# GpSimd's tensor work moved to VectorE and ScalarE, and the mixer's weights split by DMA, in a hybrid encoder layer

## The chip, the cores and the metric

The kernel runs on one core of a Trainium2 chip. The metric is the device time in microseconds, the median of three runs. The profile is one execution, taken by the hardware profiler; its times count from the first instruction.

## The reference

One layer over 512 tokens of width 1024, in float32: an input projection whose columns feed latent attention (four heads) and a gated linear recurrence in both directions (four heads, HGRN2), an output projection, a gated feed-forward of width 2816, and a gate with per-layer embeddings.

```python
h = rms_norm(x, g_mix[l]); z = h @ w_in[l]
c_q, c_kv, k_r, hq, hf_f, hf_b, hi, hg = jnp.split(z, IN_SPLITS, axis=-1)   # 256, 256, 64, then five of 512
a = mla(c_q, c_kv, k_r, cos, sin, ...)      # norms, w_qb, w_kvb, rotary parts, dense softmax
r = hgrn2(hq, hf_f, hf_b, hi, hg, ...)      # chunkwise scan per direction, chunks of 64, summed, normed, gated
x = x + jnp.concatenate([a, r], axis=-1) @ w_o[l]
h = rms_norm(x, g_ffn[l])
x = x + (silu(h @ w_gate[l]) * (h @ w_up[l])) @ w_down[l]
x = x + sigmoid(rms_norm(x, g_ple[l]) @ w_ple_gate[l]) * (p[l] @ w_ple_proj[l])
```

## The kernel before

Every large product runs as three float32r matmuls on TensorE: operands are split into a high and a low part, and `mm3` (L136 to L139) adds high x high, low x high and high x low into one PSUM bank. A chunk of weights, 128 rows by up to 1024 columns (512 KB), goes through `weights` (L143):

```python
sp.dma_start(raw[:, :cols], src)                                              # L149
split(hi[:, :cols], lo[:, :cols], raw[:, :cols], eng=lo_eng or dve)           # L150
# split without a scale:
act.activation(hi, src, AF.Copy)                                              # L130
eng.tensor_tensor(lo, src, hi, ALU.subtract)                                  # L131
```

Buffers: four raw (`RAWB`), three high and three low (`WB`). `split` with a scale (L133, L134) does the same for x and other activations on ScalarE and VectorE.

The work goes in this order.

1. *Latents of the query* (`cq`, L223): blocks of 128 features of x, eight of them, arrive one after the other with the columns of `w_q`; per block six matmuls of 512 columns. Seven warm-up matmul calls stand ahead. GpSimd sums the squares of x (L244, L246).
2. *Latents of key and value* (`ckv`, L251): a second pass over the eight blocks with `w_kv`, twelve matmuls of 320 columns per block. Then `token_rstd` makes 1/rms by token (its power runs on GpSimd, L164).
3. *Rotary tables* (L275 to L299) on GpSimd, the sines on ScalarE.
4. *Two streams side by side* (`merge`): each is a generator that yields TensorE's time piece by piece, and the one that is behind its share emits next. The latency stream has `attention()` (L329) and then the steps in the written order `LSTEPS`: per head `prepare`, `scores`, `values` of the attention, and `decays`, `within`, `carried`, `outputs`, `finish` of the recurrence. The dense stream (L868) has the input projection's other columns: `gates` for heads 0 and 1, then 2 and 3 (L598), the values (`w_in_tokens`, evacuated in L665), the embeddings, `output_gates` (L650), then half of the output projection and the embeddings' product. Its weights come through `wnext` (L560), 30 chunks in all, with one chunk ahead of use; of the first 14 every second one makes its low part on GpSimd. PSUM has eight banks, five for the latency stream and three for the dense one.
5. *The second half of the output projection, feed-forward, embeddings gate* (from L936): `weights` straight, from about 300 us to the end.

`gates(heads)` ends in a burst: sigmoids on ScalarE of six tiles of 128x512, then on VectorE f = lower + (1 - lower) sigmoid (L616), k = 1 - f (L618), two clamped copies (L627, L628), logarithms on ScalarE (L631), their sum on GpSimd (L634) and a scan on VectorE (L636, L638). `decays` has on GpSimd the distance to a chunk's middle (L681) and two products of half a tile (L698, L699). `within(h)` makes the products inside chunks, `pd` (L729), in pairs for a tile's two chunks, and per direction the one from a tile's earlier chunk to its later one, `px` (L731):

```python
for d in range(2):
    for j in range(NT):
        for c in range(2):
            pe.matmul(pd4[c * 64 : c * 64 + 64, d, j, :], ...)                # L729
        pe.matmul(px3[E * 64 : E * 64 + 64, j, :], lhsT=kx[:, j, :], ...)     # L731, E = d
```

The order of instructions on an engine is set by a planner at build time from the program's order and a simulated timeline; every engine works its list in order.

Of the kernel before, what the change touches and what calls it, by code (L numbers as in the profile page):

```python
# [8 lines left out]
F32 = mybir.dt.float32  # L9
# [6 lines left out]
P = 128  # L16
# [38 lines left out]
class Slots:  # L55
    """Tiles of one size, handed out by hand: the one that has been free longest comes next."""
# [57 lines left out]
def layer_kernel(ctx: ExitStack, tc: tile.TileContext, io, out):  # L114
# [44 lines left out]
    def rsqrt_mean(o, ss, n):  # L159
        """o = (ss / n + eps) ** -0.5, for a few columns."""  # L160
# [14 lines left out]
        # the diagonal matrices of 1 / rms, summed over the partitions  # L175
# [13 lines left out]
    def squares(acc, src, first):  # L189
        """acc += src ** 2"""  # L190
# [8 lines left out]
    # ---------------------------------------------------------------- inputs  # L199
# [3 lines left out]
    sp.dma_start(vec, io["vec"])  # L203
# [7 lines left out]
    # loads the activation engine's table while the first inputs are under way  # L211
    act.activation(small.tile([P, 1], F32, tag="first", name="first"), mhalf[:, :1], AF.Exp)
# [10 lines left out]
    for ks in ((0,), (1,), (2, 3), (4, 5), (6, 7)):  # L223
        w = weights(io["w_q"][:, ks[0] * 256 : (ks[-1] + 1) * 256], len(ks) * 256)
        for k in ks:
            if k:
                sp.dma_start(xT[k], io["xT"][k])
            split(hT[k][0], hT[k][1], xT[k], vec[:, V_MIX + k : V_MIX + k + 1])
            for m in range(2):
                o = (k - ks[0]) * 256 + m * P  # L230
                mm3(cq[m], cut(w, o, o + P), hT[k], k == 0, k == KT - 1)

    cst = cpool.tile([P, NC_], F32, name="cst")
    sp.dma_start(cst, io["cst"])
    row = cpool.tile([P, NR], F32, name="row")
    sp.dma_start(row, io["row"].partition_broadcast(P))
# [842 lines left out]
```

## Time and profile before

| | us |
|---|---|
| median of three runs (723.8 to 726.64) | 723.89 |
| profiled execution, span | 721.8 |
| TensorE busy | 703.6 (97%) |
| VectorE busy | 439.3 (61%) |
| ScalarE busy | 309.2 (43%) |
| GpSimd busy | 135.8 (19%) |

The page gives no other time of the profiled execution than its span. Matmuls are pipelined, so busy TensorE is not TensorE at its peak; the granted clock is near 1.0 in nearly all slices. PE is TensorE, PEld its weight loads, DVE VectorE, ACT ScalarE, POOL GpSimd, SP the engine that issues the transfers.

### The profile page before, as it was taken

How to read it: one execution, taken by the hardware profiler on the slowest of the kernel's cores; microseconds unless marked ns; L12 is line 12 of the kernel's file. 1: busy time of each engine (PE TensorE's matmuls, PEld its weight loads, DVE VectorE, ACT ScalarE, POOL GpSimd, SP SyncE). 2: the span in 40 equal slices, each digit the busy share in tenths (PEclk: the TensorE clock that was granted, in tenths of full speed). 3: DMA queues.
4: the chain of work that ended last, by engine and by line, in shares of the span. 5: the costliest groups of instructions: out<-in, count | busy, mean ns of one | idle time of the engine just before them, and what ended most of it. 6: DMA issues, size and time to landing. Idle time of an engine off the chain costs nothing.

```text
span 721.8 us, 9167 instructions
## 1 busy us (share of the span) xinstructions
PE 703.6 (97%) x3516; PEld 588.5 (82%) x3516; DVE 439.3 (61%) x733; ACT 309.2 (43%) x573; POOL 135.8 (19%) x126
## 2 busy tenths in 40 slices
PE   8999997998999999999999999999999999999997
PEld 6888885897878888788888888888888888888886
DVE  8954469988999984386545334435433444456573
ACT  5566785576554635355233222223222223244341
POOL 7983577010543511001000000000000000000000
PEclk9999999999999999999999999999999999999999
DMA  8432112111034221033232322232233232233211
GB/s 282 167 114 93 59 36 81 59 30 60 15 103 156 60 78 59 30 118 116 96 109 87 104 101 87 91 114 77 79 108 117 90 108 87 78 105 116 89 59 58
DMA packets 22075, 66.36 MB, mean 92 GB/s; under 512 B 2704, under 2 KB 3984, under 8 KB 22032
## 3 DMA queue, kind: packets, MB, share of 16 engines
q1 hardware_dynamic: 22032, 65.79, 28.0%
q8 instruction: 27, 0.44, 0.2%
q14 instruction: 16, 0.13, 0.1%
HBM read 63.68 MB, written 2.10 MB: 91 GB/s over the span
## 4 chain that ended last, share of the span: by engine, by line
PE 85%; DVE 8%; ACT 3%; DMA 2%; issue 1%; SPq 1%; POOL 0%; ACTq 0%; POOLq 0%
PE ff L137 11%; PE ff L138 11%; PE ff L139 11%; PE dn L138 6%; PE dn L137 6%; PE dn L139 6%; PE wi L139 3%; PE wi L137 3%; PE wi L138 3%; PE pg L139 2%; PE pg L138 2%; PE pg L137 2%; PE wo L137 2%; PE wo L139 2%; PE wo L138 2%; PE po L787 1%
## 5 line engine op out<-in xcount | busy, mean ns | idle before, releaser
L130 ACT ACTIVATE whi<-raw 128x1024 fp32r<-128x1024 f32 (+4 forms) x114 | 116.2, 1019 | 286.6 <-issue 103.1
L131 DVE TENSOR_TENSOR wlo<-raw,whi 128x1024 fp32r<-128x1024 f32 (+4 forms) x108 | 133.7, 1240 | 26.1 <-ACT whi L130 24.8
L137 PE MATMUL ff<-hh,whi 128*128 128x512 f32 x352 | 137.0, 390 | 0.1
L138 PE MATMUL ff<-hl,whi 128*128 128x512 f32 x352 | 136.8, 389 | 0.0
L139 PE MATMUL ff<-hh,wlo 128*128 128x512 f32 x352 | 136.8, 389 | 0.0
L957 DVE TENSOR_TENSOR z<-ff,rsbc 128x512 f32<-128x512 f32 x44 | 30.1, 691 | 109.8 <-PE ff L139 109.2
L164 POOL TENSOR_TENSOR rs_tok<-rs_v,mhalf 128x4 f32<-128x4 f32 x3 | 4.7, 1568 | 391.7 <-DVE rs_v L163 391.7
L137 PEld LDWEIGHTS ff<-hh,whi 128*128 128x128 f32 x352 | 66.1, 188 | 14.3 <-ACT whi L130 0.5
L138 PEld LDWEIGHTS ff<-hl,whi 128*128 128x128 f32 x352 | 66.1, 188 | 13.7
L139 PEld LDWEIGHTS ff<-hh,wlo 128*128 128x128 f32 x352 | 66.1, 188 | 13.6
L137 PE MATMUL dn<-ah,whi 128*128 128x512 f32 x176 | 68.5, 389 | 0.0
L138 PE MATMUL dn<-al,whi 128*128 128x512 f32 x176 | 68.5, 389 | 0.0
L139 PE MATMUL dn<-ah,wlo 128*128 128x512 f32 x176 | 68.5, 389 | 0.0
L139 PE MATMUL wi<-hh,wlo 128*128 128x512 f32 x128 | 51.7, 404 | 3.6 <-DVE wlo L131 3.6
L926 DVE TENSOR_TENSOR x<-x,dn 128x512 f32<-128x512 f32 x24 | 16.5, 687 | 60.5 <-PE dn L139 60.5
L138 PE MATMUL wi<-hl,whi 128*128 128x512 f32 x128 | 51.4, 401 | 0.0
L137 PE MATMUL wi<-hh,whi 128*128 128x512 f32 x128 | 51.0, 400 | 0.0
L137 PEld LDWEIGHTS dn<-ah,whi 128*128 128x128 f32 x176 | 33.0, 188 | 6.9
L139 PEld LDWEIGHTS dn<-ah,wlo 128*128 128x128 f32 x176 | 33.0, 188 | 6.8
L138 PEld LDWEIGHTS dn<-al,whi 128*128 128x128 f32 x176 | 33.0, 188 | 6.8
L139 PEld LDWEIGHTS wi<-hh,wlo 128*128 128x128 f32 x128 | 24.5, 191 | 8.9 <-DVE wlo L131 4.0
L138 PEld LDWEIGHTS wi<-hl,whi 128*128 128x128 f32 x128 | 24.4, 191 | 4.9
(287 smaller groups left out, 1361.9 us busy)
## 6 DMA issues: line engine op xcount, KB each, us to landing
raw<-in_w_gate SPq DMA_DIRECT2D x22, 512.0 KB, 3.3
raw<-in_w_up SPq DMA_DIRECT2D x22, 512.0 KB, 3.2
raw<-in_w_hf SPq DMA_DIRECT2D x16, 512.0 KB, 3.7
raw<-in_w_d SPq DMA_DIRECT2D x16, 448.0 KB, 3.2
x<-in_xT SPq DMA_DIRECT2D x16, 256.0 KB, 5.2
raw<-in_w_d SPq DMA_DIRECT2D x8, 512.0 KB, 3.3
raw<-in_w_pg SPq DMA_DIRECT2D x8, 512.0 KB, 3.2
raw<-in_w_i SPq DMA_DIRECT2D x4, 512.0 KB, 3.4
```

The lines of the kernel that those rows point to most:

```text
L130: act.activation(hi, src, AF.Copy)
L131: eng.tensor_tensor(lo, src, hi, ALU.subtract)
L137: pe.matmul(o, lhsT=l[0], rhs=r[0], start=start, stop=False)
L138: pe.matmul(o, lhsT=l[0], rhs=r[1], start=False, stop=False)
L139: pe.matmul(o, lhsT=l[1], rhs=r[0], start=False, stop=stop)
L164: pool.tensor_tensor(o, v[:, :w], mhalf[:, :w], ALU.pow)
L787: pe.matmul(po[:, ts(j)], lhsT=l, rhs=r, start=n == 0, stop=n == len(terms) - 1)
L926: dve.tensor_tensor(xT[m], xT[m], o, ALU.add)
L957: dve.tensor_tensor(z, o, bc2, ALU.mult)
```

## The change

- *GpSimd's tensor operations* go to VectorE: the rotary products of key and query, `q` times its sigmoid, the sum of logarithms, the distance to the chunk's middle, qx and kx. The squares of x are ScalarE's, their sum VectorE's. The rotary tables and the norms' powers stay on GpSimd.
- *From VectorE to ScalarE*: the evacuation of the values and the first copy of each carried state. The scale of the scores is multiplied into the query's norm, the maximum comes out negated, and the query's gains are multiplied into rotary tables of its own (`ccq`, `snq`): one operation less each time.
- *Weights of the mixer*: from the third of the 30 chunks on, GpSimd's queue issues a transfer with a cast into the high part, ScalarE writes minus the high part into the low one, and a second transfer adds the source onto it. Three chunks are asked for ahead instead of two; four high and low buffers, three raw ones. Feed-forward keeps the old way.
- *Latents together*: per block of x the weights of query and key-value come into one buffer, and the key-value matmuls of the block follow the query's; those of the last two blocks stand behind `token_rstd`. The constants are loaded in parts at other places, the rotary tables are made after the second block, ten warm-up calls instead of seven.
- *Tables*: the activation table sets are loaded by name: trigonometry first, then one set with exp and ln behind the sines and behind each group of sigmoids.
- *px in pairs*: the two directions' px of a tile are issued one behind the other.
- The dense stream emits its first four pieces ahead of the latents' evacuation.

```diff
-AHEAD = 2
-WB = 3
-RAWB = 4
+AHEAD = 3
+WB = 4
+RAWB = 3
-WARM = 7
+WARM = 10
-LO_POOL = 14
+LO_DVE = 2
+FIRST = 4
...
+        if by_dma:
+            pool.dma_start(hi[:, :cols], src)
+            act.activation(lo[:, :cols], hi[:, :cols].bitcast(F32), AF.Copy, scale=-1.0)
+            pool.dma_start(lo[:, :cols], src, accum_op=ALU.add)
+        else:
+            raw = wpool.tile([P, 1024], F32, tag="raw", bufs=RAWB, name=f"raw{nw[0]}")
+            sp.dma_start(raw[:, :cols], src)
+            split(hi[:, :cols], lo[:, :cols], raw[:, :cols])
...
+    act.preload_act_table_set("trig_and_small")
+    def exp_ln():
+        return act.preload_act_table_set("natural_log_exp_and_others")
...
+    def load_k(k):
+        if k:
+            sp.dma_start(xT[k], io["xT"][k])
...
+        sp.dma_start(raw[:, :256], io["w_q"][:, k * 256 : k * 256 + 256])
...
+        sp.dma_start(raw[:, 256:576], io["w_kv"][:, k * 320 : k * 320 + 320])
+        for c in (slice(0, 256), slice(256, 576)) if k == 0 else (slice(0, 576),):
+            split(hi[:, c], lo[:, c], raw[:, c])
+            if c.start == 0:
+                split(hT[k][0], hT[k][1], xT[k], vec[:, V_MIX + k : V_MIX + k + 1])
+        ws.append((hi, lo))
...
     for k in range(KT):
-        t = A.get("sq") if k else sq
-        pool.tensor_tensor(t, xT[k], xT[k], ALU.mult)
-        if k:
-            pool.tensor_tensor(sq, sq, t, ALU.add)
-            A.put(t)
...
+        load_k(k)
+        query_k(k)
+        if k == 1:
+            rotary_tables()
+        squares(sq, xT[k], k == 0)
+        if k < KT - 2:
+            key_k(k)
...
     rs1, bc1 = token_rstd(sq, cpool)
     A.put(sq)
+    for k in range(KT - 2, KT):
+        key_k(k)
+    BD = B.part("D", 2)
...
-            dve.tensor_scalar(rq, rq, sq_, None, ALU.mult)
+            dve.tensor_scalar(rq, rq, sq_, QK_SCALE, ALU.mult, ALU.mult)
...
-            pool.tensor_tensor(x, x, row[:, R_QN : R_QN + 64].unsqueeze(1).broadcast_to([P, H, 64]), ALU.mult)
-            rope(pool, x, x, cc[:, j : j + 1].broadcast_to([P, H, 64]),
-                 sn[:, j : j + 1].broadcast_to([P, H, 64]), t4, t8)
+            rope(dve, x, x, ccq[:, j : j + 1].broadcast_to([P, H, 64]),
+                 snq[:, j : j + 1].broadcast_to([P, H, 64]), t4, t8)
...
-            on_pool = nd[0] % 2 == 0 and nd[0] < LO_POOL
-            ahead.append(weights(*wlist.popleft(), pool if on_pool else dve))
+            ahead.append(weights(*wlist.popleft(), by_dma=nd[0] > LO_DVE))
...
-        together([lambda o=o, z=z: act.activation(o, z, AF.Sigmoid) for o, z in reversed(fs)])
+        together([lambda o=o, z=z: act.activation(o, z, AF.Sigmoid) for o, z in reversed(fs)], exp_ln)
...
-            pool.tensor_tensor(q[h], q[h], sg[h], ALU.mult)
+            dve.tensor_tensor(q[h], q[h], sg[h], ALU.mult)
...
-            pool.tensor_tensor(f, f, t, ALU.add)
+            dve.tensor_tensor(f, f, t, ALU.add)
...
-        dve.tensor_scalar(vv[j][:, cols], o, rs1[:, j : j + 1], None, ALU.mult)
+        act.activation(vv[j][:, cols], o, AF.Copy, scale=rs1[:, j : j + 1])
...
-            pool.tensor_tensor(v3(t1, 8), b3, bc8(b3[:, :, mid : mid + 1]), ALU.subtract)
+            dve.tensor_tensor(v3(t1, 8), b3, bc8(b3[:, :, mid : mid + 1]), ALU.subtract)
...
-            pool.tensor_tensor(qx, c4(e1)[:, :, L], bc4(dc[:, 0, :, L]), ALU.mult)
-            pool.tensor_tensor(kx, c4(e2)[:, :, E], bc4(dc[:, 1, :, E]), ALU.mult)
+            dve.tensor_tensor(qx, c4(e1)[:, :, L], bc4(dc[:, 0, :, L]), ALU.mult)
+            dve.tensor_tensor(kx, c4(e2)[:, :, E], bc4(dc[:, 1, :, E]), ALU.mult)
...
+            for d in range(2):
+                qx, kx = decayed[h, d][5:7]
+                pe.matmul(px3[d * 64 : d * 64 + 64, j, :], lhsT=kx[:, j, :], rhs=qx[:, j, :], start=True, stop=True)
...
+    dense = dense_stream()
+    for _ in range(FIRST):
+        next(dense)
...
+    BL = B.part("L", NBL)
+    BD.join(B)
```

## Rows read from the trace of the kernel before

**Rows 1.** Windows: stretch, its us, busy us and (count) by engine, clock, DMA, GB/s.

```profile
5.30:36.70 31.40, 28.56 (x147) 24.61 (x147) 29.91 (x29) 17.95 (x29) 30.20 (x25) 1.00 0.70 236
...
100.00:126.00 26.00, 21.41 (x91) 16.75 (x90) 24.95 (x32) 17.95 (x30) 20.37 (x14) 0.93 0.18 58
154.00:180.00 26.00, 23.22 (x147) 20.59 (x146) 21.86 (x48) 19.04 (x33) 3.81 (x3) 0.93 0.13 42
180.00:216.00 36.00, 34.59 (x234) 28.80 (x233) 33.70 (x68) 20.23 (x39) 17.91 (x13) 1.00 0.19 59
100.00:260.00 160.00, 151.18 (x932) 126.83 (x931) 149.59 (x313) 97.39 (x189) 60.91 (x46) 0.98 0.21 67
36.70:306.60 269.90, 261.04 (x1517) 219.84 (x1517) 202.17 (x432) 159.41 (x380) 100.75 (x92) 0.99 0.22 69
306.60:680.00 373.40, 373.37 (x1653) 309.36 (x1653) 181.03 (x227) 117.51 (x147) 1.93 (x1) 1.00 0.31 99
```

**Rows 2.** Timeline of 0 to 25 us: start, us, engine, line, operation, [idle before <- releaser].

```profile
1.04 3.35 PE L221 MATMUL warm<-ones 128*128 128x128 f32 x14 [1.04 <-DVE ones L206]
...
4.68 0.74 DVE L134 SCALAR_TENSOR_TENSOR hl<-x,vec,hh 128x512 fp32r<-128x512 f32 x1
...
8.90 0.63 PE L138 MATMUL cq<-hl,whi 128*128 128x512 f32 x1
...
9.33 0.63 PE L139 MATMUL cq<-hh,wlo 128*128 128x512 f32 x1
...
13.88 3.20 DVE L134 SCALAR_TENSOR_TENSOR hl<-x,vec,hh 128x512 fp32r<-128x512 f32 x2
...
15.69 0.50 PE L138 MATMUL cq<-hl,whi 128*128 128x512 f32 x1 [1.49 <-DVE hl L134]
...
24.05 0.31 PE L139 MATMUL ckv<-whi,hl 128*128 128x320 f32 x1
...
24.49 0.31 PE L139 MATMUL ckv<-whi,hl 128*128 128x320 f32 x1
```

**Rows 3.** The chain of waits, 96 to 126 and 154 to 216 us: start, us, what.

```profile
102.70 3.99 DVE z L616 x2
...
113.78 2.22 DVE wlo L131
...
176.41 1.28 ACT L631
```

**Rows 4.** Timeline of 102 to 108 us, GpSimd.

```profile
103.89 2.52 POOL L131 TENSOR_TENSOR wlo<-raw,whi 128x1024 fp32r<-128x1024 f32 x1
```

**Rows 5.** Groups by line, VectorE, 100 to 260 us: xcount | busy us, mean ns | idle before.

```profile
L131 DVE TENSOR_TENSOR wlo<-raw,whi 128x1024 fp32r<-128x1024 f32 x14 | 19.8, 1417 | 0.3 <-ACT whi L130 0.2
...
L616 DVE TENSOR_SCALAR z<-z,lower,lower 128x512 f32<-128x512 f32 x8 | 8.2, 1062 | 2.6 <-ACT z L613 2.6
...
L576 DVE TENSOR_TENSOR z<-wi,rsbc 128x512 f32<-128x512 f32 x10 | 6.7, 681 | 0.3 <-PE pT L529 0.2
...
L665 DVE TENSOR_SCALAR v<-wt,rs_tok 128x256 f32<-128x256 f32 x8 | 3.8, 475 | 2.0 <-PE av L138 1.9
...
L627 DVE TENSOR_SCALAR t<-z 128x512 f32<-128x512 f32 x8 | 3.2, 417 | 0.0
```

**Rows 6.** Groups by line, ScalarE, 36.7 to 306.6 us.

```profile
L130 ACT ACTIVATE whi<-raw 128x1024 fp32r<-128x1024 f32 x29 | 30.7, 1058 | 27.7 <-PE wo L138 10.1 <-PE wi L138 8.2 <-issue 5.8
```

**Rows 7.** Timeline of 256.2 to 257.5 us, TensorE.

```profile
256.94 0.28 PE L731 MATMUL px<-xx 128*64 128x64 f32 x2
257.06 0.28 PE L729 MATMUL pd<-e,e 128*64 128x64 f32 x2
```

**Rows 8.** DMA issues: xcount, KB each, median us to landing.

```profile
raw<-in_w_hf SPq DMA_DIRECT2D x16, 512.0 KB, 3.7
```

**Rows 9.** Groups by line, GpSimd, whole span.

```profile
L634 POOL TENSOR_TENSOR z<-z,t 128x512 f32<-128x512 f32 x8 | 13.5, 1702 | 21.9 <-ACT t L631 21.9
...
L244 POOL TENSOR_TENSOR sqacc<-x 128x512 f32<-128x512 f32 x1 | 1.0, 1038 | 2.0 <-DMA x<-in_xT 2.0
```

More of the change, by code (lines that the diff above doesn't have):

```diff
@@ L235, in layer_kernel, with together @@
     row = cpool.tile([P, NR], F32, name="row")
-    sp.dma_start(row, io["row"].partition_broadcast(P))
     pos = cpool.tile([P, NT], I32, name="pos")
-    sp.dma_start(pos, io["pos"])
     ident = cst[:, C_ID : C_ID + P]
+    ckv = [B.get(f"ckv{j}") for j in range(NT)]
+    ws = []
+    cc = cpool.tile([P, NT, 64], F32, name="cc")
+    sn = cpool.tile([P, NT, 64], F32, name="sn")
+    def together(emit, last=None):
+        es = [emit[0]()]
+        with tc.issue_after(es[0].ins):
+            for e in emit[1:]:
+                es.append(e())
+        if last:
+            with ExitStack() as behind:
+                for e in es:
+                    behind.enter_context(tc.issue_after(e.ins))
+                last()
@@ new lines, in rotary_tables @@
+    def rotary_tables():
+        posf = small.tile([P, NT], F32, tag="posf", name="posf")
+        pool.tensor_copy(posf, pos)
+        ang, rnd, tmp = (A.get(n) for n in ("ang", "rnd", "tmp"))
+        freq = cst[:, C_FREQ : C_FREQ + 32]
+        a3, n3, t3 = (t[:, : NT * 32] for t in (ang, rnd, tmp))
+        for j in range(NT):
+            pool.tensor_scalar(a3[:, j * 32 : j * 32 + 32], freq, posf[:, j : j + 1], None, ALU.mult)
+        pool.tensor_scalar(n3, a3, 1.0 / TWO_PI, None, ALU.mult)
+        pool.tensor_scalar(n3, n3, MAGIC, None, ALU.add)
+        pool.tensor_scalar(n3, n3, MAGIC, None, ALU.subtract)
+        for c in (CW1, CW2, CW3):
+            pool.tensor_scalar(t3, n3, c, None, ALU.mult)
+            pool.tensor_tensor(a3, a3, t3, ALU.subtract)
+        pool.tensor_scalar(a3, a3, 3.1415925, -3.1415925, ALU.min, ALU.max)
+        ang3 = a3.rearrange("p (a b) -> p a b", a=NT)
+        act.activation(t3, a3, AF.Abs)
+        pool.tensor_scalar(t3, t3, -1.0, TWO_PI / 4, ALU.mult, ALU.add)
+        tmp3 = t3.rearrange("p (a b) -> p a b", a=NT)
+        together([lambda: act.activation(cc[:, :, :32], tmp3, AF.Sin),
+                  lambda: act.activation(sn[:, :, 32:], ang3, AF.Sin),
+                  lambda: act.activation(sn[:, :, :32], ang3, AF.Sin, scale=-1.0)], exp_ln)
+        pool.tensor_copy(cc[:, :, 32:], cc[:, :, :32])
+        A.put(ang, rnd, tmp)
@@ L258, in layer_kernel @@
+        squares(sq, xT[k], k == 0)
+        if k < KT - 2:
+            key_k(k)
+    sp.dma_start(cst[:, :C_FREQ], io["cst"][:, :C_FREQ])
+    sp.dma_start(row, io["row"].partition_broadcast(P))
+    vlb = cpool.tile([P, 16], F32, name="vlb")
+    sp.dma_start(vlb, io["vec"][:, V_LB : V_LB + 16])
+    A.put(*xT)
     rs1, bc1 = token_rstd(sq, cpool)
     A.put(sq)
-    cT = [None] * 4
-    sqc = A.get("sqc")
-    for m in range(2):
-        cT[m] = (A.get("cTh", F32R), A.get("cTl", F32R))
-        split(cT[m][0], cT[m][1], cq[m], vec[:, V_QA + m : V_QA + m + 1])
-        squares(sqc, cq[m], m == 0)
@@ L267, in layer_kernel @@
-    B.put(*cq)
-    ctok = [A.get(f"c{j}") for j in range(NT)]
-    for j in range(NT):
-        act.copy(ctok[j][:, :320], ckv[j][:, :320])
-    B.put(*ckv)
-    BL, BD = B.part("L", NBL), B.part("D", 8 - NBL)
-    posf = small.tile([P, NT], F32, tag="posf", name="posf")
-    pool.tensor_copy(posf, pos)
-    ang, rnd, tmp = (A.get(n) for n in ("ang", "rnd", "tmp"))
-    freq = cst[:, C_FREQ : C_FREQ + 32]
-    a3, n3, t3 = (t[:, : NT * 32] for t in (ang, rnd, tmp))
-    for j in range(NT):
-        pool.tensor_scalar(a3[:, j * 32 : j * 32 + 32], freq, posf[:, j : j + 1], None, ALU.mult)
@@ L641, in gates @@
             done.add(("gates", h))
-    def together(emit):
-        first = emit[0]()
-        with tc.issue_after(first.ins):
-            for e in emit[1:]:
-                e()
     def output_gates():
@@ L655, in output_gates @@
         t = [A.get("sg") for h in range(H)]
-        together([lambda h=h: act.activation(t[h], zs[h], AF.Sigmoid) for h in reversed(range(H))])
+        together([lambda h=h: act.activation(t[h], zs[h], AF.Sigmoid) for h in reversed(range(H))], exp_ln)
         for h in range(H):
@@ L919, in layer_kernel @@
     wlist.extend((io["w_or"][c], 1024) for c in range(4))
-    merge([(latency_stream(), L_TOTAL), (dense_stream(), D_TOTAL)])
+    dense = dense_stream()
+    for _ in range(FIRST):
+        next(dense)
+    cT = [None] * 4
+    sqc = A.get("sqc")
+    for m in range(2):
+        cT[m] = (A.get("cTh", F32R), A.get("cTl", F32R))
+        split(cT[m][0], cT[m][1], cq[m], vec[:, V_QA + m : V_QA + m + 1])
+        squares(sqc, cq[m], m == 0)
+    B.put(*cq)
+    ctok = [A.get(f"c{j}") for j in range(NT)]
+    for j in range(NT):
+        act.copy(ctok[j][:, :320], ckv[j][:, :320])
+    B.put(*ckv)
+    BL = B.part("L", NBL)
+    BD.join(B)
+    merge([(latency_stream(), L_TOTAL), (dense, D_TOTAL - 1.3 * FIRST)])
     A.put(mF, *ats, *vv)
```

93 lines of the change are left out of this document (36 added, 57 removed).

## The prediction

> **What bounds the kernel now.** I read the windows by stage first, then the chain of waits inside the stages with losses, then the groups by line of the engine that the chain names, then the timeline where two engines collide. From 306.6 us on TensorE is busy without a gap: 1653 matmuls in 373.4 us, 0.226 us each, nearly all 512 columns wide [rows 1]. That stage is feed-forward, its instructions are not changed, and it returns nothing. What the change can touch lies in the first 306.6 us, and the reader is to see there how little of it is loss.
>
> The front, 5.3 to 36.7 us, holds 48 query-latent matmuls of 512 columns and 96 key-value ones of 320. At 0.226 us and 0.147 us (the latter from three starts, 24.05 to 24.49 us [rows 2]) that is 10.8 + 14.1 = 24.9 us of work in 31.4 us; 6.5 us are lost. Two causes stand in [rows 2]: at 9 us consecutive 512-column matmuls still start 0.43 us apart, which is the clock at 1.2 GHz, after a first stretch of warm-up calls with gaps behind them, and later TensorE waits 1.49 us for the low part of x that VectorE makes.
>
> The second loss is 100 to 216 us. Idle TensorE time is 26.00 - 21.41 = 4.6, 26.00 - 23.22 = 2.8 and 36.00 - 34.59 = 1.4 us, 8.8 together; and in the first two of these stages the granted clock averages 0.93, which takes 7% of 26 us, 1.8 us, from each [rows 1]: the clock fell to 1.2 GHz for a while after TensorE had waited. Sum 12.4 us. The chain of waits there runs over VectorE: two gate operations that hold it 3.99 us, a low part of weights that holds it 2.22 us [rows 3]. The timeline beside it says why they are long: GpSimd's own low part of weights runs from 103.89 for 2.52 us, to 106.41, and VectorE's two gate operations get done at 106.69, right behind it [rows 3, 4]. The same kind of gate arithmetic takes 0.42 us in another line [rows 5]. So VectorE, 149.6 of 160 us busy from 100 to 260 us [rows 1], is the engine that ends last there, and part of its busy time is waiting for GpSimd.
>
> **The change, part by part.** *Front.* Weights for query and key-value come per block of x, so that one block feeds 6 x 0.226 + 12 x 0.147 = 3.1 us of TensorE work at once instead of 1.4. VectorE then has per block a low part of 576 columns (0.77, from 0.68 at 512 wide [rows 5]), a low part of x (0.74 without contention: the smallest I see in the stretch; with it 1.60, half of the 3.20 us that two take [rows 2]) and the new square sum (0.68): 2.2 us, 3.1 with contention. ScalarE has three passes of 512 to 576 columns, of which the squares were GpSimd's before; one of 1024 columns takes 1.06 [rows 6], so I count 0.65 each, 2.0 us. TensorE stays the slowest of the three. Transfer: 256 + 288 KB per block at the 236 GB/s of this stretch [rows 1] is 2.4 us, also below 3.1. The rotary tables move forward on GpSimd, where squares no longer stand, and collide with VectorE during about four blocks; constants, row and positions are loaded a few issues later or earlier on SP, with 25 us of TensorE work as cover. The first block still pays its chain, and the three extra warm-up calls (six records of 0.24 us, 3.35 us for 14 [rows 2]) end about when the first weights arrive, so that start stays near 5.3 us. I take 2.5 us of the 6.5 as staying and 4.0 us as gain; bounds 1.5 (only the wait of 1.49 goes) and 6.0.
>
> *VectorE from 100 to 260 us.* Away go 14 low parts of weights (19.8), 8 value evacuations (3.8, now ScalarE's), the contention in the gate operations, 8 x (1.06 - 0.42) = 5.1 [rows 5], and small scalings that I don't count: 28.7 us. To it come GpSimd's 20 operations of 128x512 with two inputs at 0.68 = 13.6 and 16 of half that width at 0.45 = 7.2 (between a half and a whole one): 20.8 us. Net -8 us, 5% of 149.6, and no GpSimd tensor work beside it. The rotary products move to VectorE too, but before 100 us; outside 100 to 260 us it is busy 202.2 - 149.6 = 52.6 of 109.9 us of this part [rows 1], which hides them; without that cover each of the query's four tiles would add four operations, under 0.45 us each, 1.8 us. The loss of 100 to 126 us (4.6 + 1.8) is nearly all contention: 3.99 - 2 x 0.42 = 3.2 and 2.22 for the weight part that is no longer there, 5.4 us of chain. I give back 6.0 of 6.4. In 154 to 216 us, 6.0 us, GpSimd is little in the way (3.81 busy in 26 us [rows 1]) and the chain is VectorE's own; one of its pieces, a table load of 1.28 us for the logarithm, goes because exp and ln now share one set, loaded right behind the sigmoids [rows 3]. I give back half, 3.0. Together 9.0; bounds 3 (VectorE as full as before, only the two collisions of the first burst gone) and 12.4 (all).
>
> *px in pairs.* The px matmuls of one tile are now issued for both directions next to each other and write different halves of the partitions, as the pd pairs do already. A px call takes 0.12 us before the next pd starts [rows 7]; 32 calls, half saved: 1.9 us. Bounds 0 (hidden behind VectorE) and 1.9.
>
> *Weights by DMA.* 28 of the 30 chunks of the mixer now come by two transfers on GpSimd's queue with a ScalarE pass between: cast to the high part, minus the high part into the low one, then the source added onto it. ScalarE pays what it paid (1.06 for the high part before [rows 6]), VectorE nothing. The new waits: the adding transfer waits on GpSimd's queue for ScalarE's pass, and behind it there stand the next chunk's cast and the power operations of every norm (12 after 40 us), for which VectorE and then ScalarE's evacuations wait; the ScalarE pass waits for the cast's landing, and exponentials and PSUM evacuations stand behind it. No row shows a transfer from GpSimd's queue. Nearest is the same 512 KB by SP, 3.7 us to landing [rows 8]. Low end of one chunk's turn on the queue: 3.7 + 1.06 + two issues of 1.0 (as GpSimd's 128x512 operation alone, 1.04 [rows 9]) = 6.8 us. High end: each issue is held by VectorE as GpSimd's sums of logarithms are now (1.70 instead of 1.04 [rows 9]) or by a whole collision, seen from the other side (2.2 us of GpSimd's 2.52, taken as the other way round), and ScalarE is 1 us late: 12.2 us. Needed is a chunk every 269.9 / 28 = 9.6 us [rows 1], and 5.4 us (24 x 0.226) where TensorE has only dense work, before 57 us; there four buffers give three chunks, 16 us, of lead. I take 8 us: enough over the stretch, short by some 2.6 us for the first one or two chunks. Cost 2.0; bounds 0 and, if the turn is over 9.6 us, the rival below.
>
> A rule of the Trainium skill speaks against this part: its page "SBUF — State Buffer" (sections "SBUF: two separate sides" and "A bandwidth-pool intuition that's wrong") says that a transfer issued by GpSimd has its descriptors written by that engine, which is locked out of SBUF while VectorE runs an operation in a two-port mode, and gives about 0.6 us alone and 3.1 us beside one for such a transfer. No run here shows such a transfer yet; that the two engines hold each other up the trace agrees with (2.52 beside 3.99 us). By it, an estimate, each chunk's turn would be longer by 2 x 2.5 us, 11.8 instead of 6.8.
>
> **Sum.** 721.8 - 4.0 - 9.0 - 1.9 + 2.0 = 708.9 us for the profiled execution. The page shows no time of it but the span; the median of the runs, 723.9, is 2.1 above, which I add: **711 us**.
>
> **Rivals.** *VectorE stays the bound.* It takes on 20.8 us of GpSimd's work, and the bursts behind each sigmoid keep their length; the front gives 3.0, the middle 3.0, px 0 because it waits for VectorE, and 2.0 is paid: 717.8, 720 us with the 2.1. For it: 93% busy, and the chain of 154 to 216 us, where GpSimd is quiet; against it: the 8 us less and the two collisions that go. *GpSimd's queue becomes the bound.* Cast, wait, add, in order, longer than 9.6 us: at 10.6, 28 us over 28 chunks on top of 708.9, 739 us; it decides from about 10.1, where 0.5 x 28 = 14 us eat all gain. For it: the collisions in [rows 4], in the stretch where VectorE is fullest; against: the low end of 6.8, and that casts can be queued ahead of adds. The rule of the Trainium skill named above is this case. *TensorE alone bounds.* Every loss of the middle goes, front 6.0, px 1.9, no new wait: 721.8 - 12.4 - 6.0 - 1.9 + 2.1 = 704 us; for it, nothing but the full queues of TensorE elsewhere.
>
> **Chances.** Forecast (706 to 717) 0.58, VectorE stays 0.20, GpSimd's queue 0.13, TensorE alone 0.09. Half a per cent, 3.6 us, is about what a measurement of this kernel can tell from no change: 720.3 to 727.5. The second case straddles the lower edge, a half each side. Faster 0.58 + 0.09 + 0.10 = 0.77, same 0.10, slower 0.13. The range takes in the forecast and the two cases beside it, down to 702 (TensorE alone, with stalls shorter than a row shows) and up to 722 (VectorE stays, with 2 us more); outside is the third.
>
> **What would show it.** The profile after should have the first dense matmuls at about 33 us instead of 37; the gate operation at 0.4 to 0.6 us instead of 1.06; no TensorE stretch with granted clock below 1.0 around 116 us; VectorE below 140 us busy in the stretch that answers to 100 to 260; weight adds on GpSimd's queue less than 9.6 us apart. The forecast is wrong if TensorE waits for the low weights by name, if ScalarE idles for a landing with exponentials behind it, or if the middle's loss stays above 8 us.

## The result and the profile after

The changed kernel takes 717.29 us (median of four runs, 716.77 to 717.76), the kernel before 723.85 on the same chip: ratio 0.9897, 95% interval 0.9878 to 0.9917. It is faster by 1.0%, twice what a measurement can tell from no change. The forecast was 711 us: sign right, inside the range of 702 to 722, 0.3 us over the forecast's own band of 706 to 717, and of 12.8 us forecast 6.6 came. The profiled execution took 717.26 us with a span of 715.5.

The windows of the changed kernel, by stage (columns as in [rows 1]; the first row answers to the front, the second and third to the two bursts):

```profile
5.30:34.10 28.80, 26.93 (x155) 24.13 (x154) 24.24 (x43) 22.23 (x39) 9.91 (x18) 1.00 0.83 268
100.00:126.00 26.00, 26.00 (x123) 21.52 (x122) 25.12 (x74) 17.17 (x34) 6.77 (x9) 1.00 0.70 148
150.00:172.00 22.00, 18.16 (x88) 13.92 (x87) 20.50 (x42) 13.14 (x27) 0.00 (x0) 0.84 0.00 1
220.00:240.00 20.00, 19.38 (x100) 16.01 (x100) 15.32 (x31) 14.54 (x30) 5.19 (x7) 1.00 0.59 150
240.00:260.00 20.00, 17.53 (x167) 13.83 (x166) 14.28 (x30) 6.60 (x19) 4.11 (x6) 1.00 0.65 131
100.00:260.00 160.00, 153.07 (x987) 128.12 (x986) 127.77 (x305) 92.50 (x189) 26.28 (x35) 0.98 0.54 122
305.00:680.00 375.00, 375.00 (x1663) 310.83 (x1663) 180.02 (x230) 114.83 (x141) 3.01 (x2) 1.00 0.30 97
```

The reader is to see three things. The front is shorter and nearly full: the first dense matmul starts at 33.81 us, where it started at 37.50. From 100 to 126 us TensorE is busy without a gap at clock 1.00, where it was idle 4.6 us at 0.93 [rows 1]; VectorE is as busy there as before (25.12 of 26 us). From 150 to 172 us TensorE loses 3.8 us to idleness and runs at 0.84, and hardly a byte moves (1 GB/s); at 240 to 260 it loses 2.5 us more.

Idle time and clock can be put into one number: the time between the starts of consecutive matmuls, less the time which a matmul of that width takes in full stretches of the same trace (0.227 us for 512 columns, 0.174 for 384, 0.147 for 320, 0.118 for 256, 0.108 for 128, 0.05 for 64). Summed by stretch, in us, with e1 to e12 for the kernels of the next section (`whole` also has what lies behind 310 us, between -0.5 and 0.5):

```
stretch   before  changed   e1     e2     e4     e7     e8    e11    e12
0-50        9.1     5.8     3.9    5.3    3.6   12.7    5.5    3.2    4.8
50-100      0.4     0.4     0.4    0.3    0.4    0.4    0.4    0.4    0.4
100-150     7.5     0.4     1.4    1.5    1.0    0.4    7.9    0.4    0.7
150-180     5.3     9.1    12.5   12.2    7.9    8.8    8.4    7.2   10.1
180-220     3.6     1.3     1.2    0.9    1.3    0.1    2.7    1.6    1.6
220-310     2.5     4.4     5.5    4.2    4.3    1.2    4.2    2.2    4.0
whole      27.9    21.0    24.6   24.9    18.2   23.2   28.8   14.7   21.3
```

The changed kernel loses 6.9 us less and has six more warm-up records (0.65 us): 6.3, which is the difference of the spans, 721.8 - 715.5. By 150 us it has gained 10.4 us of lost time. Behind that it gives back 3.4.

**What the second burst looks like.** VectorE of the changed kernel, 146 to 170 us (start, us, engine, line, operation):

```profile
147.87 1.29 DVE L655 TENSOR_TENSOR z<-z,sig 128x512 f32<-128x512 f32 x2
149.08 1.91 DVE L650 TENSOR_SCALAR z<-z,lower,lower 128x512 f32<-128x512 f32 x4
...
160.69 1.27 DVE L668 TENSOR_TENSOR z<-z,t 128x512 f32<-128x512 f32 x2
...
162.27 1.28 DVE L668 TENSOR_TENSOR z<-z,t 128x512 f32<-128x512 f32 x2
163.48 1.22 DVE L672 TENSOR_TENSOR_SCAN t<-mF,z 128x512 f32<-128x512 f32 x1
164.61 0.66 DVE L132 TENSOR_TENSOR pTl<-pT,pTh 128x512 fp32r<-128x512 f32 x1
...
166.97 1.21 DVE L672 TENSOR_TENSOR_SCAN t<-mF,z 128x512 f32<-128x512 f32 x1
168.10 1.20 DVE L670 TENSOR_TENSOR_SCAN t<-mF,z 128x512 f32<-128x512 f32 x1
```

and ScalarE, in the same stretch, where L692 evacuates the values:

```profile
165.96 0.47 ACT L692 ACTIVATE v<-wt,rs_tok 128x256 f32<-128x256 f32 x1 [2.67 <-PE av L139]
166.39 0.60 ACT L131 ACTIVATE aTh<-av 128x512 fp32r<-128x512 f32 x1
168.21 0.47 ACT L692 ACTIVATE v<-wt,rs_tok 128x256 f32<-128x256 f32 x1 [1.23 <-DVE t L672]
169.33 0.47 ACT L692 ACTIVATE v<-wt,rs_tok 128x256 f32<-128x256 f32 x1 [0.64 <-DVE t L670]
```

The last low part of the probabilities (L132) stands behind the gates' work; TensorE's last attention product waits for it. The dense stream issues its last value matmul at 153.25 us and the next at 167.70: its three banks are full and are evacuated only from 166 us on. Each evacuation waits, with ScalarE idle, for work of the burst to end: the last attention product that reads `pTl`, then two of the scans. The operations that came from GpSimd are in the burst: L655 and L668, six operations, 3.8 us.

**What the weights look like.** GpSimd's queue of the changed kernel, 230 to 256 us: the adds are 8.2, 8.8 and 8.0 us apart, each with the next cast behind it.

```profile
230.53 0.87 POOL L153 DMA_DIRECT2D wlo<-in_w_oa  x1 [5.35 <-ACT st L799]
231.08 0.89 POOL L151 DMA_DIRECT2D whi<-in_w_oa  x1
238.72 0.86 POOL L153 DMA_DIRECT2D wlo<-in_w_oa  x1 [6.75 <-ACT wlo L152]
239.27 0.88 POOL L151 DMA_DIRECT2D whi<-in_w_pp  x1
247.47 0.87 POOL L153 DMA_DIRECT2D wlo<-in_w_pp  x1 [7.33 <-ACT wlo L152]
...
255.44 0.91 POOL L153 DMA_DIRECT2D wlo<-in_w_pp  x1 [5.04 <-ACT r L838]
```

ScalarE in that stretch stands 6.64 us for a cast to land; the recurrence's square sums (L824) are next in its list:

```profile
246.12 1.06 ACT L152 ACTIVATE wlo<-whi 128x1024 fp32r<-128x1024 f32 x1 [6.64 <-DMA whi<-in_w_pp]
247.09 0.26 ACT L824 ACTIVATE s<-po 128x128 f32<-128x128 f32 x1
```

The landing of these transfers (columns as in [rows 8]) and the time of their issue on GpSimd (columns as in [rows 9]):

```profile
whi<-in_w_hf POOLq DMA_DIRECT2D x14, 512.0 KB, 4.8
wlo<-in_w_hf POOLq DMA_DIRECT2D x14, 512.0 KB, 5.7
```

```profile
L153 POOL DMA_DIRECT2D wlo<-in_w_hf x14 | 13.0, 929 | 38.6 <-ACT wlo L152 38.6
L151 POOL DMA_DIRECT2D whi<-in_w_hf x14 | 9.8, 699 | 48.7 <-PE wt L140 36.3 <-PE wi L140 5.1 <-PE av L139 4.2
```

### The profile page after: what moved, and what is told of

Read it like the earlier page. It is cut to its first block, busy times and chain, and to the rows that moved or that the text cites. A ratio compares the mean times of both kernels' runs of the same rounds, so it can differ in the third digit from the quotient of the medians.

```text
span 715.5 us, 9155 instructions
## 1 busy us (share of the span) xinstructions
PE 700.5 (98%) x3522; PEld 587.3 (82%) x3522; DVE 403.9 (56%) x751; ACT 312.6 (44%) x594; POOL 70.1 (10%) x96
## 4 chain that ended last, share of the span: by engine, by line
PE 80%; issue 6%; DVE 5%; DMA 4%; ACT 2%; POOL 1%; SPq 1%; POOLq 0%; DVEq 0%; ACTq 0%
PE ff L139 11%; PE ff L138 11%; PE ff L140 11%; PE dn L138 6%; PE dn L139 6%; PE dn L140 6%; PE wi L138 3%; PE wi L139 3%; PE wi L140 3%; PE pg L140 2%; PE pg L139 2%; PE pg L138 2%; PE wo L139 1%; PE wo L140 1%; PE wo L138 1%
## 5 line engine op out<-in xcount | busy, mean ns | idle before, releaser
L131 ACT ACTIVATE whi<-raw 128x1024 fp32r<-128x1024 f32 (+1 forms) x78 | 81.1, 1040 | 259.1 <-issue 89.5
L132 DVE TENSOR_TENSOR wlo<-raw,whi 128x1024 fp32r<-128x1024 f32 (+1 forms) x78 | 93.2, 1195 | 25.6 <-ACT whi L131 24.3
L138 PEld LDWEIGHTS ff<-hh,whi 128*128 128x128 f32 x352 | 66.1, 188 | 13.8
L152 ACT ACTIVATE wlo<-whi 128x1024 fp32r<-128x1024 f32 x28 | 29.7, 1060 | 48.6 <-DMA whi<-in_w_hf 12.0
L138 PEld LDWEIGHTS wi<-hh,whi 128*128 128x128 f32 x128 | 24.1, 188 | 6.9 <-ACT sqc L199 1.3
```

The lines of the kernel that those rows point to most:

```text
L138: pe.matmul(o, lhsT=l[0], rhs=r[0], start=start, stop=False)
L152: act.activation(lo[:, :cols], hi[:, :cols].bitcast(F32), AF.Copy, scale=-1.0)
```

## The experiments

Two theories stood at the start for the second burst: VectorE's burst itself delays the attention (it took over 3.8 us of GpSimd's work there), or the value evacuations stand wrongly in ScalarE's queue. For the loss at 240 to 257 us: ScalarE's wait for a landing. Every kernel is the changed one with the edit shown. Times are medians; the ratio is to the kernel before.

```
                        us      ratio   95% interval
changed kernel        717.29   0.9897   0.9878 to 0.9917
e1 values on VectorE  720.3    0.9942   0.9929 to 0.9956
e2 weights by SP      719.25   0.9933   0.9918 to 0.9948
e3 px not in pairs    718.04   0.9906   0.9891 to 0.9921
e4 sums on GpSimd     714.39   0.9859   0.9844 to 0.9875
e5 pass later         716.27   0.9879   0.9856 to 0.9903
e6 four banks         736.44   1.0165   1.0148 to 1.0183
e7 front in 2 passes  719.53   0.9928   0.9913 to 0.9943
e8 gates on GpSimd    722.43   0.9977   0.9964 to 0.9990
e9 cast first         715.44   0.9878   0.9860 to 0.9895
e10 e9 and e4         714.35   0.9871   0.9851 to 0.9891
e11 e4 and k on ACT   711.54   0.9828   0.9813 to 0.9843
e12 six chunks by SP  717.56   0.9912   0.9898 to 0.9926
```

One limit on reading small differences: the planner undid three of the edits. The traces of e5 and e9 hold the same instructions in the same order on every engine as the changed kernel's (3522 on TensorE, 751 on VectorE, 594 on ScalarE, 96 on GpSimd), and e10's hold those of e4. So e5 and e9 are the changed kernel measured again, and e10 is e4: medians of 717.29, 716.27 and 715.44 us for the one order (716.8 over its 14 runs), 714.39 and 714.35 for the other (714.4 over 8). The stretches of one order differ too: the first 50 us lose 5.8 us in the changed kernel and about 5 and 4 in e5 and e9, 150 to 180 us lose 9.1, 9.9 and 9.8. And the losses are those of the one profiled execution, which can be slower than its kernel's median (e8: 725.36 against 722.43; e2: 721.32 against 719.25). So an edit is credited here by the stretch that it touches, and a time that differs by 2 us tells little.

**e1, the values evacuated by VectorE again.**

```diff
-        act.activation(vv[j][:, cols], o, AF.Copy, scale=rs1[:, j : j + 1])
+        dve.tensor_scalar(vv[j][:, cols], o, rs1[:, j : j + 1], None, ALU.mult)
```

> One edit undone: the values are evacuated by VectorE again, not ScalarE. In the changed kernel TensorE loses about 9 us between 150 and 170 us, and the dense stream issues no matmul from 153.25 to 167.70: its values wait in PSUM for ScalarE, whose evacuations (965.96 and 168.21 less 800, that is 165.96 and 168.21 us) stand behind a pass that waits for the attention. Theory 'ScalarE's queue': the loss of 150 to 170 us falls to 4 us or less, total 717.3 to 712-714. Rival 'VectorE's burst': VectorE is what is late there and gets 8 x 0.47 = 3.8 us more; the loss stays at 9 us or grows, total 717-721.

(The 965.96 in it is a slip of the pen; the two evacuations start at 165.96 and 168.21.) The rival held: 3.0 us slower, the loss of 150 to 180 us grows from 9.1 to 12.5, and the dense stream's stop from 14.5 to 21.2 us. On VectorE's timeline the first evacuation now stands behind the whole burst:

```profile
167.22 1.20 DVE L670 TENSOR_TENSOR_SCAN t<-mF,z 128x512 f32<-128x512 f32 x1
168.33 0.72 DVE L135 SCALAR_TENSOR_TENSOR qkl<-qkT,vec,qkh 128x512 fp32r<-128x512 f32 x1
168.97 0.86 DVE L692 TENSOR_SCALAR v<-wt,rs_tok 128x256 f32<-128x256 f32 x2
```

The move to ScalarE was a gain. The dense stream's stop changed with the loss.

**e2, no weights by GpSimd's queue.**

```diff
-LO_DVE = 2
+LO_DVE = 99
```

> One part undone: all 30 chunks of the mixer's weights come by SP's queue and are split by ScalarE and VectorE; all else as in the changed kernel. VectorE gets 28 low parts of 1.17 to 1.4 us, 33 to 39 us. Theory 'the DMA split frees VectorE and costs a wait of ScalarE': the loss of 3 us at 250 to 257 goes, but VectorE's bursts grow, 4 to 9 us lost between 100 and 170 in addition: 719-724. Rival 'the split gained nothing': the wait goes and the rest stays, 714 (717.3 - 3).

The theory held, at its lower edge: 2.0 us slower. The loss of 230 to 257 goes; of the 4.2 us left at 220 to 310, 3.1 lie behind 300, at the start of feed-forward. That of 150 to 180 grows by 3.1. Chunks split by transfers are worth about 2 us net.

The window of the first burst in e2 says more:

```profile
100.00:126.00 26.00, 26.00 (x124) 21.47 (x123) 24.88 (x69) 15.62 (x29) 0.00 (x0) 1.00 0.27 82
```

VectorE makes all low parts of weights again (four in this window, 1.21 us each), it is as full as in the kernel before (24.95 us [rows 1]), GpSimd does nothing, and TensorE has no gap. So, as far as the other parts of the change (which e2 keeps) don't bear on this window, the 4.6 us of idleness there before did not come from VectorE's low parts as such, but from GpSimd's tensor work beside them.

**e3, px as before.**

```diff
+        for d in range(2):
+            for j in range(NT):
...
+                pe.matmul(px3[d * 64 : d * 64 + 64, j, :], lhsT=kx[:, j, :], rhs=qx[:, j, :], start=True, stop=True)
```

> One edit undone: px of one direction behind that direction's pd pairs, as before the change. The prediction's term: 1.9 us slower, 719.2. From the starts of consecutive pd and px in both traces: 7.2 us before, 6.0 us after, so 1.2 us, 718.5. Rival 'hidden': no difference, 717.3.

0.75 us slower with overlapping intervals (1.2 against the 14 runs of the changed order): by its time the edit can't be told from nothing. Its trace has 7.5 us between consecutive starts of pd and px, the changed kernel's 6.0.

**e4, the second group's products and sums on GpSimd.**

```diff
-            dve.tensor_tensor(f, f, t, ALU.add)
+            (pool if heads[0] else dve).tensor_tensor(f, f, t, ALU.add)
```

(and the same for `q[h]` times `sg[h]`)

> For the second group of gates alone (heads 2 and 3) q times its sigmoid and the sums of logarithms go back to GpSimd, which is idle from 140 to 174 us. Rival 'VectorE's burst': 6 operations, 3.8 us, leave VectorE's burst, and the loss of 150 to 170 us falls by 2 to 4 us: 713.5-715.5. Theory 'ScalarE's queue': the dense stream's stop of 153 to 168 us hangs on ScalarE, change under 1.5 us: 716-718.5.

2.9 us faster, as the rival said, but by stretch only 1.2 of it lies at 150 to 180 (9.1 to 7.9), 2.2 in the first 50 us, where the edit does nothing. The direction is shown (e10, the same order, loses 7.8 there; the three measurements without the edit 9.1 to 9.9), the size expected isn't. What it costs is on the timeline: beside GpSimd's product the gate operation takes 2.49 us for three, 0.83 each, and not 0.48:

```profile
145.57 2.75 POOL L655 TENSOR_TENSOR z<-z,sig 128x512 f32<-128x512 f32 x2 [6.42 <-ACT sig L647]
146.57 2.49 DVE L650 TENSOR_SCALAR z<-z,lower,lower 128x512 f32<-128x512 f32 x3 [0.25 <-ACT z L647]
```

**e5, ScalarE's pass one request later.**

```diff
+            while late:
+                late.popleft()()
             pool.dma_start(hi[:, :cols], src)
-            act.activation(lo[:, :cols], hi[:, :cols].bitcast(F32), AF.Copy, scale=-1.0)
-            pool.dma_start(lo[:, :cols], src, accum_op=ALU.add)
+            def low():
...
+            late.append(low)
```

(`low` does the two lines taken away)

> The changed kernel with one edit: ScalarE's pass and the adding transfer of a chunk are issued when the next chunk is asked for, just ahead of its cast, so that the cast has had one chunk's time to land before ScalarE comes to the pass. In the changed kernel ScalarE stands 6.64 us at 239.5 to 246.1 for a cast to land, with the square sums of the recurrence behind it, and TensorE loses 3.2 us at 250 to 257. Theory 'ScalarE's wait for the landing': that wait and most of that loss go, 717.3 to 714-715.5. Rival 'the adds become late': TensorE waits for low weights instead, 717 or above.

716.27, overlapping with the changed kernel: neither theory was tried, since the order of instructions is the changed kernel's. GpSimd's queue and ScalarE of e5 (timeline) still show add, cast, landing, pass in one chain, 8.5 us a turn:

```profile
240.02 0.87 POOL L158 DMA_DIRECT2D wlo<-in_w_oa  x1 [6.94 <-ACT wlo L157]
240.56 0.89 POOL L154 DMA_DIRECT2D whi<-in_w_pp  x1
247.21 1.06 ACT L157 ACTIVATE wlo<-whi 128x1024 fp32r<-128x1024 f32 x1 [6.44 <-issue]
```

**e6, four banks for each stream.**

```diff
-NBL = 5
+NBL = 4
```

> The changed kernel with one number: PSUM banks are shared 4 and 4 between the latency stream and the dense one, not 5 and 3. In the changed kernel the dense stream issues nothing for 14.5 us (153.5 to 167.9) while its banks wait to be evacuated. Theory 'a bank is what the dense stream lacks in the second burst': a second pair of value tiles (48 matmuls, 5.7 us) can run there, and of the 9 us lost at 150 to 180 4 to 6 go; the latency stream loses a little elsewhere: 712-715. Rival 'VectorE's burst delays the attention and four banks choke it': the loss of 150 to 180 stays above 8 us or moves, 718-725.

The rival held: 736.44. The loss of 150 to 180 stays at 9.5 us, and 12 us are lost at 100 to 150, 4.9 of them in one wait of TensorE for the exponential that empties a bank of the scores. Whether a bank more for the dense stream alone would cure the second burst, this run doesn't tell.

**e7, the front in two passes.**

```diff
         squares(sq, xT[k], k == 0)
-        if k < KT - 2:
-            key_k(k)
+    key_k((0, 1, 2))
+    key_k((3, 4, 5))
```

(`key_k` then loads key-value weights of its own, three blocks at a time)

> One part undone: the latents of the query in a first pass over the eight blocks and those of key and value in a second one with weights of their own, as before the change; squares on ScalarE, rotary tables after the second block, warm-up, tables and everything behind as in the changed kernel. The prediction's term for the front: 4.0 us, 721.3 (bounds 1.5 to 6.0: 718.8 to 723.3). Rival 'the front's gain is lost later because the middle waits anyway': 717.3 to 718.5.

2.2 us slower: inside the bounds of the front's term, 1.8 below its number, 1.0 above the rival's range. The windows of e7, front and end of the two streams, say where the difference lies:

```profile
5.30:43.00 37.70, 31.68 (x160) 25.97 (x160) 27.65 (x56) 26.97 (x52) 13.29 (x20) 0.95 0.68 220
...
250.00:305.00 55.00, 55.00 (x363) 46.35 (x362) 27.85 (x55) 26.31 (x61) 8.70 (x11) 1.00 0.51 123
```

The front alone loses 6.9 us more (12.7 against 5.8), but 250 to 305 us has no gap, and 220 to 310 us lose 1.2 where the changed kernel loses 4.4. What the front gives is partly handed back before feed-forward. The front of e7 is not that of the kernel before, either: it loses 3.6 us more than that one (9.1), so the 6.9 us are not the price of the pairing alone.

**e8, the gates' and decays' work on GpSimd again.** Five operations (`q` times sigmoid, the sums, the distance to the middle, qx, kx) with `pool` for `dve`.

> The part that gave GpSimd's gate work to VectorE undone for both groups and the decays: q times its sigmoid, sums of logarithms, distance to the middle, qx and kx are GpSimd's again; weights still come by GpSimd's queue. VectorE gets rid of 36 operations, about 21 us. Theory 'VectorE's load in its bursts is what counts': 711-714. Rival 'GpSimd's queue': the operations wait in order among the weight transfers and hold them up, and the two engines hold each other: 718-726.

The rival held: 5.1 us slower. The groups by line of e8, VectorE at 100 to 180 us and GpSimd over the span, show why:

```profile
L672 DVE TENSOR_TENSOR_SCAN t<-mF,z 128x512 f32<-128x512 f32 x4 | 6.3, 1577 | 2.6 <-POOL z L668 2.6
...
L650 DVE TENSOR_SCALAR z<-z,lower,lower 128x512 f32<-128x512 f32 x4 | 3.1, 794 | 2.0 <-ACT z L647 2.0
...
L708 POOL TENSOR_TENSOR t<-t 128x512 f32<-128x512 f32 x8 | 10.3, 1339 | 0.0
```

The scan that takes 1.22 us alone takes 1.58, the gate operation 0.79, and VectorE also waits for GpSimd. From 100 to 150 us 7.9 us are lost, about as much as in the kernel before (7.5), although no low parts of weights are made on either engine. But it is another loss: 4.0 of the 7.9 us lie at 125 to 135 us, behind a cast that GpSimd issued at 121.73 us and that landed 7.3 us later, and the exponentials are next in ScalarE's list:

```profile
129.14 1.06 ACT L152 ACTIVATE wlo<-whi 128x1024 fp32r<-128x1024 f32 x1 [6.83 <-DMA whi<-in_w_i]
```

So both halves of the rival are in e8, the transfers held up and the engines that hold each other, and it doesn't separate them.

**e9 and e10, the cast ahead of the pass; the same with e4's edit.**

```diff
             pool.dma_start(hi[:, :cols], src)
+            while late:
+                late.popleft()()
```

> As the run that put ScalarE's pass and the adding transfer one request later, but with the next chunk's cast issued ahead of them. In that run ScalarE's passes stayed 8.2 to 8.5 us apart at 230 to 256 us (230.27, 238.67, 247.21, 255.46) with a wait of 6.4 us, since each cast still stood behind the add before it on GpSimd's queue. Theory 'order on GpSimd's queue': passes come under 6.5 us apart, ScalarE's wait for the landing falls below 2 us, most of the 3 to 4 us lost at 230 to 260 goes: 713-715 against 717.3. Rival 'the wait is not what TensorE waits for, or the adds become late': 716-718.

> The cast-first order together with the second group's products and sums of logarithms on GpSimd (that run alone: 714.4). Theory 'two separate losses, at 150 to 180 and at 240 to 257': the gains add, 711-712.5. Rival 'one of them is regained anyway': 713.5-715.

e9's 715.44 lies between its two expectations, and its interval overlaps the changed kernel's. In its trace the adds still stand ahead of the casts at 230 to 256 us (238.57 and 239.11 us), 8.2 and 7.8 us apart, and ScalarE waits 5.73 us: the written order didn't become the queue's, so the theory wasn't tried by it. e10 has e4's order and e4's time, so whether the two gains add wasn't tried either. The loss at 230 to 257 us stands in both.

**e11, e4 and k = 1 - f on ScalarE for the second group.**

```diff
-                dve.tensor_scalar(k, f, -1.0, 1.0, ALU.mult, ALU.add)
+                act.activation(k, f, AF.Identity, bias=ones[:, :1], scale=-1.0)
```

> The second group's products and sums on GpSimd as in the run that gave 714.4, and the same group's k = 1 - f on ScalarE instead of VectorE: 4 operations of 0.36 us leave VectorE's burst, 4 of about 0.6 us come to ScalarE, which is busy 13.9 of 22 us there. Theory 'VectorE's burst': the loss of 150 to 180 us (7.9) falls by 1 to 2 us, 712.5-713.8. Rival 'ScalarE becomes late with the exponentials': no gain or worse, 714-716.

711.54, better than expected, and the best of all: 1.7% below the kernel before, 0.7% below the changed one (0.9828 / 0.9897 = 0.9930). Window of e11:

```profile
150.00:172.00 22.00, 18.55 (x101) 14.79 (x100) 19.82 (x37) 15.78 (x35) 7.05 (x4) 0.92 0.01 1
```

By stretch it gains 1.9 us on the changed kernel at 150 to 180, 2.2 at 220 to 310 and 2.6 in the front; only the first is the edits' for certain, and 0.7 of it is what k on ScalarE adds to e4 (7.9 to 7.2). ScalarE was not too full for it.

**e12, chunks 21 to 26 by SP and VectorE.**

```diff
-            ahead.append(weights(*wlist.popleft(), by_dma=nd[0] > LO_DVE))
+            ahead.append(weights(*wlist.popleft(), by_dma=nd[0] > LO_DVE and not 21 <= nd[0] <= 26))
```

> The changed kernel with six chunks taken back: those of the first half of the output projection and of the embeddings' product (chunks 21 to 26 of 30) come by SP's queue and are split by ScalarE and VectorE; the other 22 stay on GpSimd's queue. VectorE is busy 29.6 of 40 us at 220 to 260 and gets 6 low parts of about 1.2 us, 7 us. Theory 'ScalarE's wait for the landing is the cost of the DMA split there': ScalarE's waits of 6.6 and 4.8 us before its passes at 246 and 254 go, the loss of 220 to 260 (3.8 us in the changed kernel) falls below 1.5 us: 713.5-715.5. Rival 'the loss is the dense stream running out of weights, or of VectorE': it stays above 2.5 us, 716.5-719.

Half right. The loss goes where the theory put it: TensorE is busy 42.00 of 42 us at 220 to 262. The time stays (717.56), because 3.3 us are lost at the start of feed-forward instead. Windows of e12:

```profile
220.00:262.00 42.00, 42.00 (x298) 35.22 (x296) 35.03 (x66) 22.04 (x50) 4.77 (x5) 1.00 0.38 113
295.00:309.00 14.00, 11.85 (x49) 8.55 (x48) 10.42 (x15) 10.20 (x16) 0.00 (x0) 1.00 0.22 75
```

and the chain of waits of e12 at that place (start, us, what):

```profile
302.11 0.68 DVE x L975
302.79 0.38 DVE hl L135
...
303.37 1.28 DVE x L975 x2
304.65 1.14 DVE wlo L132
```

The dense stream was further ahead, but the last transposes of the recurrence (rT) were done only at 291.5 us, against 289.1 in the changed kernel. TensorE reached feed-forward's first matmul 3.0 us earlier (302.0 against 305.0) and then waited for the residuals and splits that the last head starts. A loss of the dense stream that is removed while the latency stream comes no earlier turns up at the meeting point.

## Why the prediction was half right

By stretch the 6.3 us between the spans are, up to 0.1, 3.3 in the first 50 us less 0.65 for the added warm-up, 7.1 at 100 to 150, -1.5 at 150 to 220 and -1.9 at 220 to 310. The time lies in the stated range because that reaches over two rivals. The second burst came out the wrong way round; what hid part of it is that the first burst gave 1.1 us more than its term.

- **Front, 4.0 forecast.** Near in size: 3.3 us less lost in the first 50 us, less 0.65 for warm-up, inside the bounds of 1.5 to 6.0. Dense matmuls start at 33.81 us (said: about 33; before: 37.50). The prediction doesn't say how much of the term is the clock. Before, the first eleven matmuls, 5.32 to 10.16 us, are mostly 0.43 us apart, 2.3 us more in all than at 0.227; in the changed kernel the warm-up calls run right up to the first matmul, and 512 columns take 0.23 us from 6.5 us on (timeline of TensorE):

```profile
1.04 4.45 PE L231 MATMUL warm<-ones 128*128 128x128 f32 x20 [1.04 <-DVE ones L212]
...
6.52 0.39 PE L139 MATMUL cq<-hl,whil 128*128 128x512 f32 x1
6.75 0.40 PE L140 MATMUL cq<-hh,wlol 128*128 128x512 f32 x1
```

  The prediction reads the 0.43 us as the clock at 1.2 GHz; the granted clock printed for that stretch is 1.00 [rows 1], so the spacing alone shows it. No run takes the warm-up calls alone back, so the shares of warm-up and pairing are open. And e7 shows that 6.9 us lost in the front cost 2.2 at the end: the front's terms don't add one to one.
- **First burst, 6.0 forecast.** Right, 7.1 measured for 100 to 150. The gate operation takes 0.54 us instead of 1.06 [rows 5], as forecast (0.4 to 0.6), and no stretch near 116 us has a clock below 1.00. Its row in the changed kernel, groups by line, VectorE, 90 to 175 us:

```profile
L650 DVE TENSOR_SCALAR z<-z,lower,lower 128x512 f32<-128x512 f32 x8 | 4.0, 540 | 0.0
```

  That GpSimd's tensor work beside VectorE's is the cause, and not VectorE's load, is shown by e2, which keeps the rest of the change: VectorE 24.88 us of 26 busy, low parts of weights included, GpSimd silent, no gap. One piece of the reasoning falls with it: the 2.22 us of the low part in the chain needn't go, since alone it takes 1.21. e8 gives GpSimd its work back and loses 7.9 us in the stretch, but about half of that behind a late transfer. How much of the loss before is operations made longer, and how much waiting for GpSimd's slower ones, no run separates.
- **Second burst, 3.0 of 6.0 forecast as given back.** This is the step that failed. From 150 to 220 us the changed kernel loses 10.4 us, the one before 8.9: 1.5 worse instead of 3.0 better, 4.5 of the 6.6 us that are missing in the spans (12.9 forecast, 6.3 come). The step reasoned from VectorE's sum over 100 to 260 us (149.6 to 127.8 us, below the 140 that I named) and a table load that goes. The sum fell and the burst stayed full: from the first operation of the gates (147.87) to the end of the last scan (169.30) VectorE is busy 21.40 of 21.43 us. Here the rival "VectorE stays the bound" was nearer. e4 and e11 take 3.8 and about 5.2 us out of it and win back 1.2 and 1.9 us in the stretch of 150 to 180. Together the two bursts gave 5.6 of 9.0; read as the prediction reads it (idle time and clock, 100 to 216 us), 7.4 us stay, just under the 8 that I named as a sign of being wrong.
- **What the loss hangs on besides.** The loss of 150 to 180 us rises with the dense stream's longest stop, loosely: 5.3 us at a stop of 9.5 (before), 7.2 at 11.9 (e11), 7.9 at 13.8 (e4), 9.1 at 14.5 (changed), 12.2 at 15.6 (e2), 12.5 at 21.2 (e1); but at stops of 14.3 and 14.4 it is 8.4 (e8) to 10.8 (e3), and 8.8 at 12.3 (e7). The stop ends when a bank is evacuated, and what the evacuations wait for is not their place in a list. They start at 165.96, 168.21 and 169.33 us, 0.03 to 0.04 us behind the end of the last product that reads `pTl` and of two scans, and they read nothing that these make. What ties them is the buffer that they write: the values take theirs from the first-in, first-out list of 74 that all such tiles share. Following that list through the program, the first two values get the buffers of two gate tiles `z`, which the scans read last, and the third that of a `pTl`. So after 72 value matmuls three full banks wait for buffers that the burst still holds. In the kernel before, the first value got the buffer of a sigmoid, was evacuated at 161.56 us, and 96 value matmuls came before the stop. The forecast has no term for this. It is read from code and traces; no run gave the values other buffers, so how much of the loss hangs on it is open.
- **px, 1.9 forecast.** Too large by the traces: between consecutive starts of pd and px they show 7.2 us before and 6.0 after, 1.2 us. e3's time doesn't settle it.
- **Weights by transfers, 2.0 forecast as cost.** The turn of a chunk was right (8 us; 8.0 to 8.8 measured at 230 to 256 us, below the 9.6 needed on average), its place wrong. The first chunks came nearly in time: 40 to 50 us loses 0.9 us in the changed kernel and 0.03 to 0.7 in e1, e3, e4, e5 and e8. The price is paid at 230 to 257 us, where ScalarE stands for the landing, the sign that I had named for being wrong, with square sums behind it and not exponentials: 3.6 us, against 0.4 in the kernel before. e12 removes it without gain, and e2, the whole part undone, is 2.0 us slower, so the part as a whole helps. That 220 to 310 us is 1.9 us dearer and 2.0 were forecast is luck.
- **The rule on GpSimd's descriptors.** The issues take 0.70 and 0.93 us in the mean, the longest of the changed kernel 1.21; at 100 to 126 us, with VectorE 97% busy, none takes over 1.11. The Trainium skill, page "SBUF — State Buffer", section "A bandwidth-pool intuition that's wrong", gives about 0.6 us alone and 3.1 beside such an operation; no issue here comes near the second figure, and the rows don't tell which of VectorE's operations ran in a two-port mode. By the Trainium skill, page "Perfetto Trace Analysis", section "DMA Instruction — SWDGE (GPSIMD)", the end that a profile shows for such an issue is the end of writing descriptors; a wait ahead of the span's start would not be seen in it. But the turn would: 11.8 us was the estimate by the rule, 8.0 to 8.8 were measured, and the measurement decides.

## What to carry to other kernels

Work moved to an engine is to be costed in the stretch where it lands: VectorE's sum over 100 to 260 us fell by 22 us, and its second burst still had no gap. Where the operations of two engines make each other longer, moving the work onto one can win even when that one is already full (100 to 126 us: 24.95 of 26 us before, 25.12 after), and moving it apart again in one burst can win where the other engine is idle (e4, e11). A buffer from a shared list can tie a product to work that it has nothing to do with: look at what an evacuation waits for before giving it another engine or place. With two streams that meet, a loss removed in the one pays only as far as the other comes earlier too (e7, e12).

## What the runs showed that I had not expected

- A tensor operation of GpSimd beside VectorE lengthens not only gate operations (0.54 to 0.79 us, e8) but scans too (1.22 to 1.58 us), and GpSimd's own subtraction of 128x512 takes 1.34 us there, where VectorE takes 0.68 in the changed kernel.
- A transfer on GpSimd's queue of 512 KB lands after 4.8 us with the cast and 5.7 us with the addition, against 3.7 for the plain one by SP [rows 8].
- One PSUM bank taken from the latency stream and given to the dense one costs 19 us (e6).
